# One-hot factors of the expert gates: eight tokens per instruction, in pairs of tokens, all on VectorE

## The chip, the cores and the metric

The kernel runs on one core of a Trainium2 chip. The metric is the device time of one execution in microseconds. Three runs of the kernel before gave 2724.03, 2725.5 and 2726.63 us (median 2725.5). All times below that are not totals come from one profiled execution of it.

## The reference, cut to what matters

The program is a two-layer transformer over 256 latent tokens and 256 context tokens. Each layer ends in a mixer of experts ("PEER"): for each token, eight heads pick 16 of 128 x 128 single-neuron experts, so that a token has 128 picks, each with an expert number and a gate.

```python
idx = (i1 * PEER_NKEYS + i2).reshape(T, PEER_HEADS * PEER_TOPK)
g = jax.nn.softmax(fv, axis=-1).reshape(T, PEER_HEADS * PEER_TOPK)
...
ue = u[ic]
ve = v[ic]
act = jax.nn.gelu(jnp.einsum('td,ted->te', hc, ue), approximate=False)
return jnp.einsum('te,ted->td', gc * act, ve)
```

i1 and i2 are the first and the second key of an expert, each 0 to 127. The kernel gathers rows of u and v for only 128 of the layer-0 tokens. For the other tokens (384 in layer 0, 256 in layer 1) it computes all 16384 experts densely, and multiplies by a dense table of gates that is zero where a token didn't pick an expert.

## The kernel before, in words

That dense table is made by `dense_gates`, once for each block of 128 tokens: three passes in layer 0, two in layer 1. For one token the table of 128 x 128 gates is a product of two matrices over the token's 128 picks: one row per pick that is one-hot in the second key (tile `oh2`, from i2), and one row per pick that holds the pick's gate at the place of the first key and zero elsewhere (tiles `go`). The gate is kept as two bf16 parts, x = 0 and x = 1, so each token takes two matmuls of 128x128 that add up in PSUM.

The first key's one-hot row is itself an outer product: n1 = 8 a + b, with a from 0 to 15 and b from 0 to 7. `one_hots(b)` makes, for 16 tokens, the one-hot of a (`hot0`, line 707), the one-hot of b (`hot1`, line 707), and `gh` = one-hot of a times either part of the gate (line 711). In `hot0`, `hot1` and `gh` the 16 tokens are the innermost dimension. Then for each group of eight tokens line 723 makes `oh2` in one VectorE instruction of 1024 elements per partition (four pairs of tokens x 128 keys x 2), and line 730 makes `go` by four instructions for each gate part, one for each pair of tokens, 256 elements per partition each. It reads two adjacent tokens out of every 16 of `hot1`. The instructions of part x = 1 go to GpSimd for the first `pools` groups of every 16 tokens, which `SHARE` sets by block: two of two in the first pass, none in the second, third and fifth, one of two in the fourth. That is 96 instructions on GpSimd and 544 on VectorE.

TensorE does the 16 matmuls of eight tokens (line 739) into two PSUM banks, ScalarE copies each bank to the tile `stage` (line 741), and after 16 tokens SyncE's queue writes `stage` to HBM as 1 MB (line 742). `oh2`, `go` and `stage` have two buffers each.

The five passes don't run alone. `dense` is the loop over the 128 rows of experts. Its first half, `first(i)`, loads 512 KB of u, splits it into two bf16 parts (ScalarE line 100, VectorE line 101), projects all tokens onto it with 24 matmuls (line 281) and applies Gelu (line 766). The results of the first 28 rows in layer 0 and the first 48 in layer 1 have places to be kept (four more buffers rotate), so these `first` steps may run while the gates are still being made. The second half, `second(i)`, needs the finished table (tile `gq`, read back from HBM). The routing of the next block (`route`: lines 620 to 670, all on VectorE) also lies within a pass. The order of all instructions on an engine is set at build time by a scheduler that works with its own estimate of costs; at run time every engine goes through its own list in order.

Of the kernel before, what the change touches and what calls it, by code (L numbers as in the profile page):

```python
# [10 lines left out]
BF = mybir.dt.bfloat16  # L11
# [22 lines left out]
NK = 128  # L34
# [7 lines left out]
TB = 16  # L42
OCT = 8
OHT = 8


@with_exitstack
def program(ctx: ExitStack, tc: tile.TileContext, a, out):
    nc = tc.nc
    V, A, T, G = nc.vector, nc.scalar, nc.tensor, nc.gpsimd  # L50
# [624 lines left out]
    def iota_tables(gp):  # L675
        row = load("iota", [P, NK], a["iota"], pool=gp)
        t = gp.tile([P, NK, 2], BF, name="iotaT")
        V.tensor_copy(t, row.unsqueeze(2).to_broadcast([P, NK, 2]))
        t16 = gp.tile([P, 16, TB], BF, name="iota16T")
        V.tensor_copy(t16, row[:, :16].unsqueeze(2).to_broadcast([P, 16, TB]))  # L680
        return t, t16

    def dense_gates(ii, gate, tb0, gd, gp, tables, steps, pools=2):
# [17 lines left out]
        def one_hots(b):  # L701

            bs = slice(b * TB, (b + 1) * TB)
            hot = []
            for x, n in ((0, 16), (1, 8)):
                o = gp.tile([P, n, TB], BF, name=f"hot{x}", bufs=2)
                V.tensor_tensor(o, iota16[:, :n], iT[:, x, bs].unsqueeze(1).to_broadcast([P, n, TB]), op=OP.is_equal)
                hot.append(o)
            gh = gp.tile([P, 2, 16, TB], BF, name="gh", bufs=2)
            for x in range(2):  # L710
                V.tensor_tensor(gh[:, x], hot[0], gT[:, x, bs].unsqueeze(1).to_broadcast([P, 16, TB]), op=OP.mult)  # L711
            return hot[1], gh

        ahead = one_hots(0)
        for b in range(P // TB):
            stage = gp.tile([P, NK, TB], F32, name="stage", bufs=2)
            (low, gh), ahead = ahead, one_hots(b + 1) if b < P // TB - 1 else None
            for t8 in range(TB // OHT):

                ts = slice(b * TB + t8 * OHT, b * TB + (t8 + 1) * OHT)  # L720
                pairs = [P, OHT // 2, NK, 2]
                oh = gp.tile(pairs, BF, name="oh2", bufs=2)
                V.tensor_tensor(oh, iota.unsqueeze(1).to_broadcast(pairs),  # L723
                                iT[:, 2, ts].rearrange("p (q t) -> p q t", t=2).unsqueeze(2).to_broadcast(pairs), op=OP.is_equal)
                go = []
                for x in range(2):
                    o = gp.tile([P, OHT // 2, 16, 8, 2], BF, name=f"go{x}", bufs=2)
                    for q in range(OHT // 2):
                        t = t8 * OHT + 2 * q
                        (G if x == 1 and t8 < pools else V).tensor_tensor(  # L730
                            o[:, q], gh[:, x, :, t:t + 2].unsqueeze(2).to_broadcast([P, 16, 8, 2]),
                            low[:, :, t:t + 2].unsqueeze(1).to_broadcast([P, 16, 8, 2]), op=OP.mult)
                    go.append(o.rearrange("p q a b t -> p q (a b) t"))
                for t4 in range(0, OHT, 4):
                    p = bank(("sc", "pv")[t4 // 4])
                    for t in range(4):
                        q, r = (t4 + t) // 2, t % 2
                        for x in range(2):
                            T.matmul(p[:, t * NK:(t + 1) * NK], oh[:, q, :, r], go[x][:, q, :, r], start=(x == 0), stop=(x == 1))  # L739
# [92 lines left out]
    with ExitStack() as layer0:  # L832
        with ExitStack() as es:
# [8 lines left out]
            with tc.issue_after(mod_last[0].ins):  # L842
                r = rms_of((CTXS, XS))
# [3 lines left out]
            steps = modulation(0, (2, 3, 4), sc, f0, f0)  # L847
# [24 lines left out]
        for g in range(2):  # L872
            p = bank("tr")
# [4 lines left out]
        gd = tc.dram_tile([P, NK // OCT, 3 * P // TB, OCT * TB], F32, name="gd0")  # L878
        with ExitStack() as gstack:
            gp = pool("gates0", gstack, 1, side="right")  # L880
            tables = iota_tables(gp)
            picks = []
            advance(route(best[2], rp, rank, rp, "", picks), 13)
            advance(ctx_scores, 1)
            advance(x_scores, 6)
            for b, after in ((2, 0), (0, 1), (1, 3)):
                following = []
                steps = route(best[after], rp, rank, *((keep, "3") if after == 3 else (rp, "")), following)
                dense_gates(*picks, b * P // TB, gd, gp, tables, chain(x_scores, steps), SHARE[b])
# [107 lines left out]
    with ExitStack() as layer1:  # L997
# [13 lines left out]
        with ExitStack() as gstack:  # L1011
            gp = pool("gates1", gstack, 1, side="right")
            tables = iota_tables(gp)
            picks, following = [], []
            advance(route(best[0], rp, rank, rp, "", picks), 13)
            advance(scores, 1)
            dense_gates(*picks, 0, gd, gp, tables, route(best[1], rp, rank, rp, "", following), SHARE[3])
            dense_gates(*following, P // TB, gd, gp, tables, iter(()), SHARE[4])
        right.close()
        dp = pool("dp1", layer1, 2, side="right")  # L1020

# [153 lines left out]
```

## Time and profile before

| | us |
|---|---|
| median of three runs | 2725.5 |
| the profiled execution | 2726.53 |
| its span in the trace | 2724.8 |
| layer 0: first, second, third pass of the gates (533 to 643, 643 to 723, 723 to 796) | 110, 80, 73 |
| layer 1: first, second pass (1987 to 2094, 2094 to 2163) | 107, 69 |

The span runs from the first instruction to the last; the 1.7 us between it and the execution's time lie outside of the trace. The boundaries of the stretches are read from the chain of waits: a pass begins with its first `oh2` and its last stretch ends when its gates are written. A busy time adds up the time in which at least one instruction of a group runs. Since two VectorE instructions overlap a little where one follows the other directly, the step from one start to the next is shorter than a duration; the pieces of the chain show these steps.

### The profile page before, as it was taken

The numbers are of one execution on the slowest core, as the hardware profiler recorded it, in microseconds if no ns is written. First come the engines' busy times: TensorE is split into PE (matmuls) and PEld (weight loads), VectorE is DVE, ScalarE is ACT, GpSimd is POOL, SyncE is SP. The second block draws the span as 40 slices with busy tenths as digits, with TensorE's granted clock in tenths as the row PEclk, the third lists the DMA queues.
The fourth block names the chain that finished last, engine by engine and source line by source line (L and its number), as shares of the span: only waits on it lengthen the run. The fifth ranks groups of instructions, "written<-read, shape, count | busy, mean of one in ns | idle before, by whom it ended". The sixth has DMA issues, their size and how long they took to land.

```text
span 2724.8 us, 42285 instructions
## 1 busy us (share of the span) xinstructions
PE 2490.9 (91%) x15465; PEld 1588.5 (58%) x15600; DVE 2246.9 (82%) x5284; ACT 1222.3 (45%) x2117; POOL 317.4 (12%) x228
## 2 busy tenths in 40 slices
PE   6999999989559999999999998898988599999998
PEld 2866489655334455555555555667877444666665
DVE  6975659999999999999898886967998897666665
ACT  3235535434333443344443334555554345555554
POOL 0000000160000122332322210000043000000000
PEclk8989899989659999999999999899999699999999
DMA  7621225455569899999999863603566787767762
GB/s 259 220 75 36 87 99 178 128 163 171 147 232 350 327 370 369 359 400 382 373 363 356 332 220 117 222 1 101 175 188 200 238 284 266 245 218 233 233 218 84
DMA packets 221005, 614.13 MB, mean 225 GB/s; under 512 B 16758, under 2 KB 104312, under 8 KB 199804
## 3 DMA queue, kind: packets, MB, share of 16 engines
q1 hardware_dynamic: 202364, 477.19, 51.4%
q0 software_dynamic: 18432, 134.23, 12.6%
q8 instruction: 122, 2.00, 0.3%
q14 instruction: 87, 0.71, 0.1%
HBM read 565.21 MB, written 46.15 MB: 224 GB/s over the span
## 4 chain that ended last, share of the span: by engine, by line
PE 66%; DVE 24%; DMA 4%; issue 3%; ACT 2%; POOL 1%; SPq 0%; DVEq 0%; ACTq 0%; POOLq 0%
PE tr L281 21%; PE sc L789 10%; PE pv L789 10%; PE mm L281 7%; DVE go L730 6%; PE mm L789 6%; DVE half L101 5%; DMA v<-in_v 2%; PE sc L384 2%; DVE oh L723 2%; PE tr L291 1%; PE pv L548 1%; PE mm L319 1%; PE sc L531 1%; PE sc L319 1%
## 5 line engine op out<-in xcount | busy, mean ns | idle before, releaser
L281 PEld LDWEIGHTS <-half 128*128 128x128 bf16 x7488 | 727.3, 99 | 291.9 <-issue 15.2
L281 PE MATMUL tr<-h,half 128*128 128x384 bf16 (+1 forms) x6144 | 885.4, 301 | 3.2 <-ACT ga L766 1.6
L789 PEld LDWEIGHTS <-wh 128*128 128x128 bf16 x2560 | 251.0, 98 | 317.3 <-ACT wh L781 35.2
L101 DVE TENSOR_TENSOR half<-u,half 128x1024 bf16<-128x1024 f32 (+1 forms) x300 | 368.9, 1231 | 70.2 <-ACT half L100 69.6
L774 DVE TENSOR_TENSOR vv<-v,vv 128x1024 bf16<-128x1024 f32 x256 | 312.0, 1220 | 98.0 <-ACT vv L773 97.4
L773 ACT ACTIVATE vv<-v 128x1024 bf16<-128x1024 f32 x256 | 268.9, 1054 | 259.2 <-DMA v<-in_v 84.6
L100 ACT ACTIVATE half<-u 128x1024 bf16<-128x1024 f32 (+1 forms) x300 | 315.0, 1050 | 100.7 <-DMA u<-in_u 36.2
L907 POOL DMA_INDIRECT uv<-in_uv,idx x128 | 201.2, 1572 | 780.9 <-DVE acc L919 458.8
L789 PE MATMUL pv<-vv,wh 128*128 128x512 bf16 x956 | 255.0, 381 | 40.5 <-ACT wh L781 33.8
L789 PE MATMUL sc<-vv,wh 128*128 128x512 bf16 x994 | 266.2, 381 | 2.0 <-issue 0.4
L766 ACT ACTIVATE ga<-tr 128x384 f32<-128x384 f32 (+1 forms) x230 | 100.1, 435 | 307.9 <-PE tr L281 305.1
L730 POOL TENSOR_TENSOR go<-gh,hot 128x256 bf16<-128x256 bf16 x96 | 116.0, 1239 | 976.8 <-DVE gh L711 932.3
L789 PEld LDWEIGHTS <-wl 128*128 128x128 bf16 x1280 | 125.4, 98 | 151.0 <-issue 0.8
L159 DVE CUSTOM_DVE_ANT_0 junk<-wm,silu_c 128x1024 bf16<-128x1024 f32 x160 | 194.6, 1216 | 4.1 <-DMA wm<-in_w_mod 3.1
L730 DVE TENSOR_TENSOR go<-gh,hot 128x256 bf16<-128x256 bf16 x544 | 191.9, 413 | 0.0
L779 DVE TENSOR_TENSOR wf<-ga,gq 128x384 f32<-128x384 f32 (+1 forms) x230 | 111.6, 489 | 92.8 <-ACT ga L766 81.0
L739 PEld LDWEIGHTS <-oh 128*128 128x128 bf16 x1280 | 106.5, 114 | 133.2 <-DVE oh L723 42.9
L781 ACT ACTIVATE wh<-wf 128x384 bf16<-128x384 f32 (+1 forms) x256 | 117.8, 462 | 144.5 <-DVE wf L779 93.0
L919 DVE SCALAR_TENSOR_TENSOR acc<-uv,wgt,acc 128x1024 f32<-128x1024 f32 x127 | 162.4, 1279 | 1.9
L913 DVE CUSTOM_DVE_ANT_0 uv<-uv,ht 128x1024 f32<-128x1024 f32 x128 | 155.4, 1215 | 2.7 <-DMA uv<-in_uv,idx 2.7
L789 PE MATMUL pv<-vv,wl 128*128 128x512 bf16 x508 | 152.0, 380 | 0.3
L789 PE MATMUL sc<-vv,wl 128*128 128x512 bf16 x508 | 151.4, 379 | 0.2
(274 smaller groups left out, 3005.3 us busy)
## 6 DMA issues: line engine op xcount, KB each, us to landing
u<-in_u SPq DMA_DIRECT2D x256, 512.0 KB
v<-in_v SPq DMA_DIRECT2D x256, 512.0 KB
wm<-in_w_mod SPq DMA_DIRECT2D x80, 512.0 KB
gd<-stage SPq DMA_DIRECT2D x40, 1024.0 KB
gq<-gd SPq DMA_DIRECT2D x16, 1536.0 KB
gq<-gd SPq DMA_DIRECT2D x16, 1024.0 KB
u<-in_w_pq SPq DMA_DIRECT2D x24, 512.0 KB
v<-in_w_pq SPq DMA_DIRECT2D x24, 512.0 KB
```

The costliest lines, as they stand in the source:

```text
L100: A.activation(h, t, AF.Copy)
L101: V.tensor_tensor(l, t, h, op=OP.subtract)
L159: mod_last[0] = order(V.tensor_tensor_reduce(junk, w, sc[:, s], 1.0, 0.0, OP.mult, OP.add, mods[layer][:, k, j, s:s + 1]))
L281: T.matmul(p[:, :n], w[i][:, c], src[j][:, c, t0:t0 + n], start=(c == 0 and i + j == 0), stop=(c == NC - 1 and i == 1))
L730: (G if x == 1 and t8 < pools else V).tensor_tensor(o[:, q], gh[:, x, :, t:t + 2].unsqueeze(2).to_broadcast([P, 16, 8, 2]), low[:, :, t:t ...
L773: A.activation(vh, v, AF.Copy)
L774: V.tensor_tensor(vl, v, vh, op=OP.subtract)
L781: A.activation(wh, wf, AF.Copy)
L789: T.matmul(acc[t][x], w[:, s], v[:, x * 512:(x + 1) * 512], start=(i == 0 and w is wh and v is vh), stop=(i == NK - 1 and w is wl))
L907: dma = G.indirect_dma_start(out=uv[:], out_offset=None, in_=a["uv0"], in_offset=bass.IndirectOffsetOnAxis(ap=idx[:, k:k + 1], axis=0))
L913: keep_order(V.tensor_tensor_reduce(uv[:, :D], uv[:, :D], ht, 1.0, 0.0, OP.mult, OP.add, act3[:, k:k + 1]))
L919: V.scalar_tensor_tensor(acc3, uv[:, D:], wgt3[:, k:k + 1], acc3, op0=OP.mult, op1=OP.add)
```

## The change

`one_hots(n)` now works for 32 tokens (`QUART`) and in five-dimensional tiles. `gh` is laid out as groups of eight tokens: [group, a, token]; its one-hot of a is written in place and multiplied there, so three instructions of 512 elements per partition replace the six of 256 that 32 tokens took (`hot0` and `gh`). The one-hot of b, now `low`, is laid out as [pair of tokens, b, token of the pair], by one instruction of 256 elements for 32 tokens. `go` is one tile for both gate parts, and each part of eight tokens comes from one instruction of 1024 elements. That instruction goes through a, the pairs, b and the token of a pair; it reads the eight tokens' part of `low` as one run of 64 elements, again for each a, and writes runs of 16 elements that lie 256 elements apart. All of them are on VectorE; `SHARE` and `pools` go. The one-hots are no longer made one block of 16 tokens ahead in the code. Matmuls, copies and writes are the same.

```diff
-        t16 = gp.tile([P, 16, TB], BF, name="iota16T")
-        V.tensor_copy(t16, row[:, :16].unsqueeze(2).to_broadcast([P, 16, TB]))
+        t16 = gp.tile([P, 16, OHT], BF, name="iota16T")
+        V.tensor_copy(t16, row[:, :16].unsqueeze(2).to_broadcast([P, 16, OHT]))
...
-            hot = []
-            for x, n in ((0, 16), (1, 8)):
-                o = gp.tile([P, n, TB], BF, name=f"hot{x}", bufs=2)
-                V.tensor_tensor(o, iota16[:, :n], iT[:, x, bs].unsqueeze(1).to_broadcast([P, n, TB]), op=OP.is_equal)
-                hot.append(o)
-            gh = gp.tile([P, 2, 16, TB], BF, name="gh", bufs=2)
-            for x in range(2):
-                V.tensor_tensor(gh[:, x], hot[0], gT[:, x, bs].unsqueeze(1).to_broadcast([P, 16, TB]), op=OP.mult)
-            return hot[1], gh
...
+            ns = slice(n * QUART, (n + 1) * QUART)
+            wide, pairs = [P, QUART // OHT, 16, OHT], [P, QUART // 2, 8, 2]
+            group = lambda x: x.rearrange("p (g t) -> p g t", t=OHT).unsqueeze(2).to_broadcast(wide)
+            gh = gp.tile([P, 2] + wide[1:], BF, name="gh", bufs=2)
+            V.tensor_tensor(gh[:, 0], iota16.unsqueeze(1).to_broadcast(wide), group(iT[:, 0, ns]), op=OP.is_equal)
+            V.tensor_tensor(gh[:, 1], gh[:, 0], group(gT[:, 1, ns]), op=OP.mult)
+            V.tensor_tensor(gh[:, 0], gh[:, 0], group(gT[:, 0, ns]), op=OP.mult)
+            low = gp.tile(pairs, BF, name="low", bufs=2)
+            V.tensor_tensor(low, iota[:, :8].unsqueeze(1).to_broadcast(pairs),
+                            iT[:, 1, ns].rearrange("p (q t) -> p q t", t=2).unsqueeze(2).to_broadcast(pairs), op=OP.is_equal)
+            return gh, low
...
-                    o = gp.tile([P, OHT // 2, 16, 8, 2], BF, name=f"go{x}", bufs=2)
-                    for q in range(OHT // 2):
-                        t = t8 * OHT + 2 * q
-                        (G if x == 1 and t8 < pools else V).tensor_tensor(
-                            o[:, q], gh[:, x, :, t:t + 2].unsqueeze(2).to_broadcast([P, 16, 8, 2]),
-                            low[:, :, t:t + 2].unsqueeze(1).to_broadcast([P, 16, 8, 2]), op=OP.mult)
-                    go.append(o.rearrange("p q a b t -> p q (a b) t"))
+                    V.tensor_tensor(go[:, x].rearrange("p q (a b) t -> p a q b t", b=8),
+                                    gh[:, x, g].rearrange("p a (q t) -> p a q t", t=2).unsqueeze(3).to_broadcast(outer),
+                                    low[:, g * nq:(g + 1) * nq].unsqueeze(1).to_broadcast(outer), op=OP.mult)
```

The scheduler's lists change with it. On VectorE, in the middle of the third pass, eight tokens stand as follows before. The names are those of the code, with `oh` for the one-hot of the second key and `fv`, `fi`, `rest` of the routing of the next block:

```order
L730 TENSOR_TENSOR go_6860<-gh,hot_6713 128x256
L723 TENSOR_TENSOR oh_6858<-iotaT,iT 128x1024
L730 TENSOR_TENSOR go_6860<-gh,hot_6713 128x256 x3
L730 TENSOR_TENSOR go_6865<-gh,hot_6713 128x256 x2
L630 MAX_INDEX fi<-fv,rest_6613 128x8
L730 TENSOR_TENSOR go_6865<-gh,hot_6713 128x256 x2
```

In the changed kernel sixteen tokens of the same pass stand like this (`gh` and `low` here are the next 32 tokens' one-hots, the lines 637 and 651 the routing):

```order
L728 TENSOR_TENSOR oh_6458<-iotaT,iT 128x1024
L733 TENSOR_TENSOR go<-gh,low 128x16x4x16 x2
L637 TENSOR_REDUCE gs<-gate 128x8
L709 TENSOR_TENSOR gh<-iota16T,iT 128x512
L713 TENSOR_TENSOR low<-iotaT,iT 128x256
L651 CAST atf<-at 128x128
L728 TENSOR_TENSOR oh_6483<-iotaT,iT 128x1024
L733 TENSOR_TENSOR go<-gh,low 128x16x4x16 x2
```

Eight `go` instructions of eight tokens became two; the scheduler still makes the next 32 tokens' one-hots before they are due. On VectorE in the last pass, 16 tokens before (line 101 is the split of u for two `first` steps):

```order
L723 TENSOR_TENSOR oh_20219<-iotaT,iT 128x1024
L730 TENSOR_TENSOR go_20221<-gh,hot_20141 128x256 x3
L730 TENSOR_TENSOR go_20226<-gh,hot_20141 128x256 x4
L723 TENSOR_TENSOR oh_20251<-iotaT,iT 128x1024
L730 TENSOR_TENSOR go_20253<-gh,hot_20141 128x256 x4
L730 TENSOR_TENSOR go_20258<-gh,hot_20141 128x256 x4
L707 TENSOR_TENSOR hot_20358<-iota16T,iT 128x256
L101 TENSOR_TENSOR half<-u_23491,half 128x1024
L101 TENSOR_TENSOR half<-u_23546,half 128x1024
```

And now:

```order
L728 TENSOR_TENSOR oh_19614<-iotaT,iT 128x1024
L733 TENSOR_TENSOR go<-gh,low 128x16x4x16 x2
L728 TENSOR_TENSOR oh_19639<-iotaT,iT 128x1024
L733 TENSOR_TENSOR go<-gh,low 128x16x4x16 x2
L102 TENSOR_TENSOR half<-u_22771,half 128x1024
L709 TENSOR_TENSOR gh<-iota16T,iT 128x512
L713 TENSOR_TENSOR low<-iotaT,iT 128x256
```

The splits of u keep their places between the groups: from the first `oh2` of a pass to that of the next, or to the table's end, VectorE's list holds 16, 11, 0, 25 and 10 of them before, and 18, 9, 0, 24 and 11 now. TensorE's list holds 386 and 183 of the 128x384 projections in the first two passes before, 429 and 118 now, none in the third in either; in the fourth pass 571 of the 128x256 ones before and 544 now.

## Rows read from the trace of the kernel before

**Rows 1.** The page: busy time, share of the span and instruction count of each engine over the whole program, and the granted TensorE clock in 40 equal slices of the span, in tenths of full speed.

```profile
PE 2490.9 (91%) x15465; PEld 1588.5 (58%) x15600; DVE 2246.9 (82%) x5284; ACT 1222.3 (45%) x2117; POOL 317.4 (12%) x228
...
PEclk8989899989659999999999999899999699999999
```

**Rows 2.** Five stretches, which are the five passes of dense_gates with what lies in front of them. Columns: the stretch and its length in us; busy us (and instructions) of PE, PEld, DVE, ACT and POOL; granted TensorE clock as a share of full speed; mean busy share of the DMA engines; GB/s.

```profile
533.00:643.00 110.00, 94.12 (x664) 59.92 (x663) 109.79 (x364) 46.27 (x72) 59.45 (x64) 0.91 0.52 154
643.00:723.00 80.00, 60.99 (x466) 39.62 (x464) 79.90 (x251) 33.02 (x51) 0.00 (x0) 0.85 0.60 174
723.00:796.00 73.00, 36.20 (x258) 26.10 (x258) 72.67 (x277) 24.08 (x39) 0.00 (x0) 0.50 0.45 128
1987.00:2094.00 107.00, 87.71 (x816) 72.97 (x813) 97.28 (x233) 52.41 (x84) 56.56 (x32) 0.90 0.65 197
2094.00:2163.00 69.00, 52.79 (x483) 42.79 (x480) 66.70 (x188) 31.89 (x54) 0.00 (x0) 0.77 0.67 199
```

**Rows 3.** The chain of waits between 640 and 732 us: its shares by line, and five of its pieces in order of time (start us, us on the chain, engine, tile, line, and xN where N instructions follow each other).

```profile
by line: DVE go L730 45.9%; DVE half L101 12.5%; DVE oh L723 11.3%; DVE gh L711 4.3%; issue 3.5%; DVE hot L707 3.3%; DVE oh L669 2.5%; DVE oh L666 2.5%; DVE rest L628 1.7%; DVE fi L630 1.6%; DVE fi L627 1.6%; DVE oh L665 1.3%; DVE fv L626 1
...
641.92 0.53 DVE hot L707 x3
...
644.50 1.14 DVE half L101
645.63 0.60 DVE gh L711 x3
...
711.72 0.60 DVE oh L723
712.32 2.70 DVE go L730 x9
```

**Rows 4.** The chain of waits between 1984 and 2168 us, the passes of layer 1: its shares by line, and the last write of gates to HBM.

```profile
by line: DVE go L730 33.0%; DVE half L101 15.3%; POOL go L730 10.0%; DVE oh L723 9.4%; PE tr L281 9.2%; issue 4.7%; DVE gh L711 3.4%; DVE hot L707 3.3%; DMA gd<-stage 2.9%; PE sc L739 1.9%; PE pv L739 1.8%; DVE fi L627 0.8%; DVE fi L630 0.7
...
2162.15 5.25 DMA gd<-stage
```

**Rows 5.** VectorE's groups by line between 533 and 623 us, the first pass. Columns: line, engine, operation, out<-in, shapes, count | busy us, mean ns of one | idle us before.

```profile
L730 DVE TENSOR_TENSOR go<-gh,hot 128x256 bf16<-128x256 bf16 x64 | 31.4, 536 | 0.0
L101 DVE TENSOR_TENSOR half<-u,half 128x1024 bf16<-128x1024 f32 x12 | 16.5, 1375 | 0.0
L723 DVE TENSOR_TENSOR oh<-iotaT,iT 128x1024 bf16<-128x1024 bf16 x16 | 12.2, 762 | 0.0
L711 DVE TENSOR_TENSOR gh<-hot,gT 128x256 bf16<-128x256 bf16 x16 | 7.8, 520 | 0.0
L707 DVE TENSOR_TENSOR hot<-iota16T,iT 128x128 bf16<-128x128 bf16 (+1 forms) x13 | 5.7, 442 | 0.0
```

**Rows 6.** The same columns for VectorE between 1987 and 2094 us, the fourth pass.

```profile
L730 DVE TENSOR_TENSOR go<-gh,hot 128x256 bf16<-128x256 bf16 x96 | 37.5, 443 | 0.0
L101 DVE TENSOR_TENSOR half<-u,half 128x1024 bf16<-128x1024 f32 x25 | 32.5, 1305 | 9.6 <-ACT half L100 9.6
L723 DVE TENSOR_TENSOR oh<-iotaT,iT 128x1024 bf16<-128x1024 bf16 x16 | 11.2, 706 | 0.0
L707 DVE TENSOR_TENSOR hot<-iota16T,iT 128x256 bf16<-128x256 bf16 (+1 forms) x14 | 4.9, 353 | 0.0
L711 DVE TENSOR_TENSOR gh<-hot,gT 128x256 bf16<-128x256 bf16 x16 | 3.8, 277 | 0.0
```

**Rows 7.** Instructions in order of time around 2055 us, merged: start us, us, engine, line, operation, count [idle before <- what ended it].

```profile
2055.18 20.23 POOL L730 TENSOR_TENSOR go<-gh,hot 128x256 bf16<-128x256 bf16 x4 [5.85 <-DVE gh L711]
...
2073.63 1.08 PE L739 MATMUL sc<-go,oh 128*128 128x128 bf16 x7 [8.83 <-POOL go L730]
...
2079.47 1.22 DVE L101 TENSOR_TENSOR half<-u,half 128x1024 bf16<-128x1024 f32 x1 [6.41 <-ACT half L100]
```

**Rows 8.** Line 730 over the whole program: engine, operation, count: duration in ns, shortest/median/longest, first and last start.

```profile
L730 DVE TENSOR_TENSOR go<-gh,hot x544: 327/381/847, 536.9 to 2160.3; 128x256 bf16<-128x256 bf16 x182
L730 POOL TENSOR_TENSOR go<-gh,hot x96: 642/802/18402, 535.3 to 2074.8; 128x256 bf16<-128x256 bf16 x96
```

**Rows 9.** TensorE's groups by line and shape between 533 and 643 us, columns as in rows 5.

```profile
L281 PE MATMUL tr<-h,half 128*128 128x384 bf16 x388 | 70.6, 342 | 0.0
L739 PE MATMUL pv<-go,oh 128*128 128x128 bf16 x128 | 13.6, 241 | 6.0 <-DVE go L730 5.9
L739 PE MATMUL sc<-go,oh 128*128 128x128 bf16 x128 | 13.1, 241 | 9.9 <-DVE oh L723 5.1 <-DVE go L730 4.6
```

**Rows 10.** TensorE in order of time between 639 and 653 us, merged (start us, us, count); a group of eight matmuls can show seven here, the other one standing apart or missing.

```profile
639.67 7.15 PE L281 MATMUL tr<-h,half 128*128 128x384 bf16 x43
...
651.11 0.64 PE L739 MATMUL pv<-go,oh 128*128 128x128 bf16 x7
651.72 0.63 PE L739 MATMUL sc<-go,oh 128*128 128x128 bf16 x7
```

**Rows 11.** The same for the fifth pass, in layer 1.

```profile
2104.04 4.53 PE L281 MATMUL tr<-h,half 128*128 128x256 bf16 x40
```

**Rows 12.** ScalarE's split of the streamed u weights (line 100) between 1987 and 2094 us, columns as in rows 5.

```profile
L100 ACT ACTIVATE half<-u 128x1024 bf16<-128x1024 f32 x24 | 25.3, 1054 | 19.9 <-DMA u<-in_u 14.5 <-DVE go L730 2.2 <-DVE gh L711 2.1
```

More of the change, by code (lines that the diff above doesn't have):

```diff
@@ L44 @@
 OHT = 8
+QUART = 32
 @with_exitstack
@@ L678, in iota_tables, with dense_gates @@
         V.tensor_copy(t, row.unsqueeze(2).to_broadcast([P, NK, 2]))
-        t16 = gp.tile([P, 16, TB], BF, name="iota16T")
-        V.tensor_copy(t16, row[:, :16].unsqueeze(2).to_broadcast([P, 16, TB]))
+        t16 = gp.tile([P, 16, OHT], BF, name="iota16T")
+        V.tensor_copy(t16, row[:, :16].unsqueeze(2).to_broadcast([P, 16, OHT]))
         return t, t16
-    def dense_gates(ii, gate, tb0, gd, gp, tables, steps, pools=2):
+    def dense_gates(ii, gate, tb0, gd, gp, tables, steps):
         iota, iota16 = tables
@@ L699, in dense_gates @@
         V.tensor_tensor(gT[:, 1], p[:, 3 * P:], gT[:, 0], op=OP.subtract)
-        def one_hots(b):
-            bs = slice(b * TB, (b + 1) * TB)
-            hot = []
-            for x, n in ((0, 16), (1, 8)):
-                o = gp.tile([P, n, TB], BF, name=f"hot{x}", bufs=2)
-                V.tensor_tensor(o, iota16[:, :n], iT[:, x, bs].unsqueeze(1).to_broadcast([P, n, TB]), op=OP.is_equal)
-                hot.append(o)
-            gh = gp.tile([P, 2, 16, TB], BF, name="gh", bufs=2)
-            for x in range(2):
-                V.tensor_tensor(gh[:, x], hot[0], gT[:, x, bs].unsqueeze(1).to_broadcast([P, 16, TB]), op=OP.mult)
-            return hot[1], gh
@@ L714, in dense_gates, with one_hots @@
-        ahead = one_hots(0)
+        def one_hots(n):
+            ns = slice(n * QUART, (n + 1) * QUART)
[9 more added lines that the diff above has]
+            return gh, low
@@ L715, in dense_gates @@
+        nq = OHT // 2
         for b in range(P // TB):
             stage = gp.tile([P, NK, TB], F32, name="stage", bufs=2)
-            (low, gh), ahead = ahead, one_hots(b + 1) if b < P // TB - 1 else None
+            if b % (QUART // TB) == 0:
+                gh, low = one_hots(b // (QUART // TB))
             for t8 in range(TB // OHT):
[L720 to L725, printed above, removed]
-                for x in range(2):
-                    o = gp.tile([P, OHT // 2, 16, 8, 2], BF, name=f"go{x}", bufs=2)
-                    for q in range(OHT // 2):
-                        t = t8 * OHT + 2 * q
-                        (G if x == 1 and t8 < pools else V).tensor_tensor(
-                            o[:, q], gh[:, x, :, t:t + 2].unsqueeze(2).to_broadcast([P, 16, 8, 2]),
-                            low[:, :, t:t + 2].unsqueeze(1).to_broadcast([P, 16, 8, 2]), op=OP.mult)
-                    go.append(o.rearrange("p q a b t -> p q (a b) t"))
@@ new lines, in dense_gates @@
+                g = b * (TB // OHT) + t8
+                ts = slice(g * OHT, (g + 1) * OHT)
+                g %= QUART // OHT
+                shape = [P, nq, NK, 2]
+                oh = gp.tile(shape, BF, name="oh2", bufs=2)
+                V.tensor_tensor(oh, iota.unsqueeze(1).to_broadcast(shape),
+                                iT[:, 2, ts].rearrange("p (q t) -> p q t", t=2).unsqueeze(2).to_broadcast(shape), op=OP.is_equal)
+                go = gp.tile([P, 2] + shape[1:], BF, name="go", bufs=2)
@@ L734, in dense_gates @@
+                outer = [P, 16, nq, 8, 2]
+                for x in range(2):
+                    V.tensor_tensor(go[:, x].rearrange("p q (a b) t -> p a q b t", b=8),
+                                    gh[:, x, g].rearrange("p a (q t) -> p a q t", t=2).unsqueeze(3).to_broadcast(outer),
+                                    low[:, g * nq:(g + 1) * nq].unsqueeze(1).to_broadcast(outer), op=OP.mult)
                 for t4 in range(0, OHT, 4):
@@ L738, in dense_gates @@
                         for x in range(2):
-                            T.matmul(p[:, t * NK:(t + 1) * NK], oh[:, q, :, r], go[x][:, q, :, r], start=(x == 0), stop=(x == 1))
+                            T.matmul(p[:, t * NK:(t + 1) * NK], oh[:, q, :, r], go[:, x, q, :, r], start=(x == 0), stop=(x == 1))
                     ts0 = t8 * OHT + t4
@@ L820, in program @@
     PRE = (18, 32)
-    SHARE = {2: 2, 0: 0, 1: 0, 3: 1, 4: 0}
     PARKED = (TT * NC // (3 * P), TT * NC // SEQ)
@@ L888, in program @@
                 steps = route(best[after], rp, rank, *((keep, "3") if after == 3 else (rp, "")), following)
-                dense_gates(*picks, b * P // TB, gd, gp, tables, chain(x_scores, steps), SHARE[b])
+                dense_gates(*picks, b * P // TB, gd, gp, tables, chain(x_scores, steps))
                 picks = following
@@ L1016, in program @@
             advance(scores, 1)
-            dense_gates(*picks, 0, gd, gp, tables, route(best[1], rp, rank, rp, "", following), SHARE[3])
-            dense_gates(*following, P // TB, gd, gp, tables, iter(()), SHARE[4])
+            dense_gates(*picks, 0, gd, gp, tables, route(best[1], rp, rank, rp, "", following))
+            dense_gates(*following, P // TB, gd, gp, tables, iter(()))
         right.close()
```

## The prediction

> **What bounds the kernel now.** I read the page first. Over the whole program TensorE is busy 91% and VectorE 82% [rows 1], which names TensorE; but the change touches only the five passes that make the gates, so I cut these out by windows. [...] In layer 1 line 730 has 33%, GpSimd's share of the same line 10% and TensorE's projections 9% [rows 4]. [...]
>
> **Prices.** On the bounding engine I count from one start to the next, as the chain does: `go` 2.70 / 9 = 0.30 us, `oh2` 0.60, `gh` 0.60 / 3 = 0.20, `hot` 0.53 / 3 = 0.18, a split of u 1.14 [rows 3]. A duration is some 0.08 us more, since neighbours overlap.
>
> The new `go` has 1024 bf16 elements, as `oh2` has. `oh2` too holds a pair of one source over many steps, reads the other as a run and takes 0.60. I take 0.60, the nearest row; it is the lower end too, as no two-source row passes more elements in a time. The upper end is one element at a time: the split of u, also 1024 elements but partly fp32, 1.14.
>
> What speaks for the dearer end is that the old `go` takes 0.30 where `gh`, of the same size and type, takes 0.20 [rows 3]: something in its access costs 0.10 us over 128 pairs. [...] No run here has yet shown which of the streams pays.
>
> The one-hots of 512 elements aren't in the trace. They lie between 0.20 (256) and 0.60 (1024); on the line between these 0.33. The ends would change a pass by -1.6 or +3.2 us.
>
> **One pass, VectorE alone.** Before, without GpSimd: 128 `go` x 0.30 + 16 `oh2` x 0.60 + 16 `gh` x 0.20 + 16 `hot` x 0.18 = 38.4 + 9.6 + 3.2 + 2.9 = 54.1. After: 32 x 0.60 + 16 x 0.60 + 12 x 0.33 + 4 x 0.20 = 19.2 + 9.6 + 4.0 + 0.8 = 33.6. That is 20.5 us less.
>
> **What VectorE then needs, pass by pass** (the new list has 18, 9, 0, 24 and 11 splits of u where there were 16, 11, 0, 25 and 10).
> - First: GpSimd had half of `go`, but everything on VectorE ran longer beside it: 64 `go` at 536 ns, `gh` at 520, `oh2` at 762, splits at 1375 [rows 5], where the median of all `go` is 381 [rows 8]. The four groups' 57.1 us less 109 overlaps of 0.08 are 48.4; 33.6 replace them, -14.8. The splits fall back to 1.22: 12 x 0.155 = -1.9. Two more splits: +2.3. 110 - 14.4 = 95.6.
> - Second: 80 - 20.5 - 2 x 1.14 = 57.2. Third: 73 - 20.5 = 52.5.
> - Fourth: 57.4 us in the four groups less 142 x 0.08 are 46.0 [rows 6], so -12.4; splits 25 x 0.085 = -2.1; one split less -1.1. Here one GpSimd `go` lasted 18.4 us, 0.64 at best [rows 8]: TensorE stood 8.8 us for it and VectorE afterwards 6.4 in one piece [rows 7], 9.6 in all [rows 6]. That goes too: 107 - 25.2 = 81.8.
> - Fifth: 69 - 20.5 + 1.1 = 49.6.
>
> **What is late next.** TensorE's work doesn't shrink. A 128x384 projection takes 7.15 / 43 = 0.166 us at the full clock, a 128x256 one 4.53 / 40 = 0.113, eight gate matmuls 0.61 from one group's start to the next [rows 10, 11], so a pass's 32 groups 19.5. First pass: the new list's 429 projections x 0.166 + 19.5 = 91; before, their 70.6 us and the gates' 27 filled most of the 110 [rows 9]. Second 39, third 20 (39 at half clock), fourth 544 x 0.113 + 19.5 = 81, fifth 264 x 0.113 + 19.5 = 49. In the second and third VectorE stays alone. In the first, fourth and fifth the two are equal within 5%, and two engines that feed each other through two buffers don't both run full.
>
> The transfers come closer as well. In the fourth pass ScalarE already waits 14.5 us for u [rows 12] at a DMA share of 0.65 [rows 2]; in 90 us that share is 0.77. At the end of the fifth pass no split is left, VectorE needs 33.6 / 8 = 4.2 us for 16 tokens, and the write of their 1 MB takes 5.25 us [rows 4] out of two buffers: I let three or four such groups take a microsecond more each.
>
> So I take 98 (95.6 + 2), 58, 53, 90 (82 + 8 for u and TensorE) and 57 (50 + 4 for the writes + 3 for u): 356 us instead of 439, 83 less. What is behind the passes has the same matmuls in the same number but for a projection step or two, and is TensorE's [rows 1]; I count nothing there. The profiled execution took 2726.5 us (1.0 above the median of 2725.5): 2726.5 - 83 = **2643 us**.
>
> GpSimd's 96 instructions cost nothing by their absence; its gathers come later and aren't moved. ScalarE and the copies are as before. The loss of the written look-ahead costs nothing where the list has the next one-hots early, as it has; where it hasn't, two or three dependent instructions per 32 tokens wait for each other, within the "issue" share of 3.5% [rows 3].
>
> **The rivals.**
> - *VectorE's sum is all there is.* The scheduler's list happens to keep TensorE and u in step: 95.6 + 57.2 + 52.5 + 81.8 + 49.6 = 337, -102, 2624 us. For it: TensorE has filled such stretches well. Against it: three passes with two equal limits. 14%.
> - *Layer 1 gives nothing,* because u, the 1 MB writes and TensorE hold it where it is: 98 + 58 + 53 + 107 + 69 = 385, -54, 2672 us. For it: the 14.5 us wait, TensorE busy 88 of 107. Against it: most of that busy time is matmuls in a pipeline that waits, and the 18 us GpSimd instruction goes anyway. 16%.
> - *One element at a time:* `go` at 1.14 adds 160 x 0.54 = 86; some 17 of that are hidden under the allowances above: 2726.5 - 83 + 86 - 17 = 2712. Against it `oh2`, which has the same dimensions. 5%.
> - *Slower: the hop price on every stream.* If the 0.10 us per 128 pairs is paid by both sources and the output (whose runs are 256 elements apart), 512 pairs pay 3 x 0.40, `go` costs 1.80, and 160 x 1.20 - 17 = 175 more give 2818. The change loses from `go` = 0.60 + (83 + 17) / 160 = 1.22 on. For it: the old price is unexplained by the trace. Against it: `gh` and `oh2` are free of it. 4%.
> - *Nothing moves:* the passes wait for something that the chain doesn't name, within 0.2% of before. 2%.
>
> **How the numbers follow.** My forecast, 2626 to 2662 (the allowances halved or doubled), has 59%. The range takes in the two neighbours: 2610 to 2685; what is left out is mainly the dear `go` and luck beyond. Two runs of this kernel can be told apart by about 0.2%, 5.5 us. Faster by more: 59 + 14 + 16 + 5 = 94%; within: 2%; slower: 4%.
>
> **What would show it.** Right: `go` x160 at about 660 to 680 ns; `gh` at 0.40 or so; nothing of line 730's successor on GpSimd; the third pass, free of projections, at 53 us with VectorE full; the first and fourth with both engines over 90%. Wrong: `go` above 0.8; a third pass above 60, which would mean that dependences between VectorE and TensorE and not VectorE's work set it; TensorE idle behind u in layer 1; a dense stage that became longer by what the passes gave.

## The result and the profile after

The changed kernel takes 2623.8 us (median of four runs, 2620.2 to 2627.2) where the kernel before, on the same chips, takes 2725.1: a ratio of 0.9626, with a 95% interval of 0.9614 to 0.9638. That is 101 us less. The forecast was 2643 us within 2610 to 2685; the measured time lies on the first rival, VectorE's bare sum of 2624.

The page, beside [rows 1]: busy time by engine, and the granted clock in 40 slices.

```profile
PE 2454.3 (94%) x15600; PEld 1570.8 (60%) x15600; DVE 2142.3 (82%) x4820; ACT 1218.7 (46%) x2117; POOL 196.4 (7%) x132
...
PEclk8989899999679999999999999999999899999999
```

TensorE's share rises from 91 to 94% because the span is shorter; GpSimd's busy time falls by the 116 us of `go` and a little more. The stretch of the third pass, which stood at a granted 0.50 in [rows 2], has 0.61 in the window below.

The five passes by windows, beside [rows 2], same columns. The cuts are put at the new places of each pass's first `oh2`:

```profile
534.00:625.00 91.00, 88.30 (x708) 59.07 (x706) 90.86 (x321) 47.69 (x75) 0.00 (x0) 1.00 0.66 198
625.00:686.00 61.00, 49.84 (x430) 35.73 (x428) 60.90 (x168) 31.07 (x51) 0.00 (x0) 0.86 0.68 201
686.00:738.00 52.00, 29.06 (x256) 23.99 (x256) 49.91 (x139) 20.96 (x35) 0.00 (x0) 0.61 0.66 186
1928.00:2010.00 82.00, 79.24 (x825) 70.82 (x824) 75.05 (x155) 50.86 (x84) 0.00 (x0) 0.98 0.83 257
2010.00:2066.00 56.00, 42.83 (x477) 38.18 (x475) 50.24 (x80) 32.89 (x54) 0.00 (x0) 0.91 0.87 264
```

VectorE is still full in layer 0, and TensorE is at 88 of 91 us beside it in the first pass. In the fourth and fifth VectorE stands for 7 and 6 us, and the DMA share has gone from 0.65 and 0.67 to 0.83 and 0.87.

The new `go` over the whole program, beside [rows 8] (count: shortest/median/longest ns), and the first of the three instructions that make `gh`:

```profile
L733 DVE TENSOR_TENSOR go<-gh,low x160: 673/682/692, 539.8 to 2056.2; 128x1024 bf16<-128x1024 bf16 x160
```

```profile
L709 DVE TENSOR_TENSOR gh<-iota16T,iT x20: 397/412/424, 534.0 to 2039.3; 128x512 bf16<-128x512 bf16 x20
```

160 instructions at a median of 682 ns, where `oh2` has 681 for as many elements, and 512 elements in 412 ns: the prices 0.60 and 0.33 from start to start that the forecast used. The chain at the end of the third pass shows the steps, beside [rows 3] (start us, us on the chain, piece):

```profile
by line: DVE go L733 35.7%; DVE oh L728 17.7%; DMA gq<-gd 12.8%; DMA gd<-stage 10.8%; DVE fi L631 2.9%; DVE gh L709 2.4%; DVE gh L710 2.4%; DVE gh L711 2.3%; DVE rest L629 2.1%; DVE oh L670 2.1%; DVE oh L667 2.1%; DVE oh L666 2.1%; ACT stag
...
726.32 0.60 DVE oh L728
726.92 1.21 DVE go L733 x2
728.32 0.60 DVE oh L728
728.92 1.22 DVE go L733 x2
...
732.24 5.81 DMA gd<-stage
738.11 6.94 DMA gq<-gd
```

Two `go` are 1.20 to 1.22 us, `oh2` 0.60. The pass now ends with the last write and the read back, where VectorE's routing used to be the last thing.

For a comparison pass by pass I use the same cuts everywhere: from a pass's first `oh2` to the next pass's first `oh2`, and for the third and fifth to the issue of the first read of `gq`. "Sum" is the forecast's bare VectorE sum (-14.4, -22.8, -20.5, -25.2, -19.4) on these cuts.

| pass | before, us | sum, us | after, us |
|---|---|---|---|
| 1 | 109.5 | 95.1 | 90.0 |
| 2 | 82.4 | 59.6 | 61.8 |
| 3 | 69.0 | 48.5 | 51.5 |
| 4 | 108.3 | 83.1 | 81.9 |
| 5 | 72.3 | 52.9 | 55.7 |
| all | 441.5 | 339.2 | 340.9 |

So 100.6 us of the 102.5 by which the span shrank come from these passes. Between them and behind them nothing was given back: from the first read of `gq` in layer 0 to the first `oh2` of layer 1 it is 1193.4 us before and 1190.7 after.

### The profile page after: what moved, and what is told of

Its sections match the earlier page's. It is cut to its first block, busy times and chain, and to the rows that moved or that the text cites. A ratio compares the mean times of both kernels' runs of the same rounds, so it can differ in the third digit from the quotient of the medians.

```text
span 2622.3 us, 41821 instructions
## 1 busy us (share of the span) xinstructions
PE 2454.3 (94%) x15600; PEld 1570.8 (60%) x15600; DVE 2142.3 (82%) x4820; ACT 1218.7 (46%) x2117; POOL 196.4 (7%) x132
## 4 chain that ended last, share of the span: by engine, by line
PE 71%; DVE 19%; DMA 5%; issue 2%; ACT 2%; SPq 0%; DVEq 0%; ACTq 0%
PE tr L282 23%; PE sc L791 12%; PE pv L791 12%; PE mm L282 8%; PE mm L791 6%; DVE half L102 4%; DVE go L733 3%; PE sc L385 2%; PE tr L292 2%; DVE oh L728 1%; PE pv L549 1%; PE mm L320 1%; PE sc L320 1%; PE sc L532 1%; DMA u<-in_u 1%
## 5 line engine op out<-in xcount | busy, mean ns | idle before, releaser
L791 PE MATMUL pv<-vv,wh 128*128 128x512 bf16 x1024 | 269.7, 382 | 35.2 <-ACT wh L783 32.1
L282 PE MATMUL mm<-h,half 128*128 128x256 bf16 (+1 forms) x1248 | 137.4, 271 | 11.1 <-ACT h L274 3.5
L282 PE MATMUL mm<-hT,half 128*128 128x512 f32 (+1 forms) x672 | 140.1, 362 | 6.6 <-ACT hT L274 3.1
L791 PE MATMUL mm<-vv,wh 128*128 128x512 bf16 x512 | 134.4, 381 | 0.0
```

The lines of the kernel that those rows point to most:

```text
L282: T.matmul(p[:, :n], w[i][:, c], src[j][:, c, t0:t0 + n], start=(c == 0 and i + j == 0), stop=(c == NC - 1 and i == 1))
L791: T.matmul(acc[t][x], w[:, s], v[:, x * 512:(x + 1) * 512], start=(i == 0 and w is wh and v is vh), stop=(i == NK - 1 and w is wl))
```

## The experiments

Nine kernels were run. All medians are of runs beside the kernel before on the same chip, which took 2726.3 to 2727.3 us there.

### GpSimd's part alone

The kernel before, with all of line 730 on VectorE:

```diff
-    SHARE = {2: 2, 0: 0, 1: 0, 3: 1, 4: 0}
+    SHARE = {2: 0, 0: 0, 1: 0, 3: 0, 4: 0}
```

> The kernel before with all of line 730 on VectorE and nothing else changed. Theory A (the gain is VectorE's own: the price of one go): the first pass gains 64 go x 0.30 on VectorE and loses GpSimd's interference, 54.1 in place of 48.4 and splits 1.9 less, +4; the fourth 54.1 in place of 46.0, splits 2 less, the 9.6 us stall gone, -4. In all 2725 us, within 8. Rival B (what the change won is mostly GpSimd's interference and its 18 us instruction): 40 to 60 us of the 101 come from this alone, 2665 to 2685.

Measured 2712.5 us, ratio 0.9956 (0.9942 to 0.9970): 14 us faster than the kernel before. That is far from rival B, but 12 us below theory A's 2725 and outside the 8 that it allowed. The duration of `go` hardly moves against [rows 8], while VectorE does 96 more of them:

```profile
L730 DVE TENSOR_TENSOR go<-gh,hot x640: 330/385/475, 535.3 to 2148.9; 128x256 bf16<-128x256 bf16 x160
```

The passes tell where. The scheduler's list now has 21, 6, 0, 26 and 9 splits of u in the passes. With 1.14 us for each split more or less and the price of `go` as forecast, they should take 119.0, 76.7, 69.0, 105.8 and 71.2 us; measured are 114.4, 76.6, 69.1, 102.1 and 71.1. Passes two, three and five agree within 0.1 us. The first and fourth, the two with GpSimd, are 4.6 and 3.7 us shorter than reckoned: the forecast had taken VectorE's work beside GpSimd too low (why is said further down).

```profile
535.00:649.00 114.00, 103.72 (x768) 66.43 (x767) 113.76 (x432) 51.77 (x80) 0.00 (x0) 1.00 0.57 171
1987.00:2089.00 102.00, 90.48 (x875) 76.06 (x873) 97.97 (x267) 53.42 (x88) 0.00 (x0) 0.98 0.72 217
```

The windows of these two passes show VectorE full at 113.8 of 114 us and 98.0 of 102 even without it (columns as in [rows 2]). In the fourth it still waits 4.0 us behind u:

```profile
L101 DVE TENSOR_TENSOR half<-u,half 128x1024 bf16<-128x1024 f32 x26 | 31.2, 1213 | 4.0 <-ACT half L100 4.0
```

### GpSimd's part given back to the changed kernel

```diff
-                    V.tensor_tensor(go[:, x].rearrange("p q (a b) t -> p a q b t", b=8),
+                    (G if x == 1 and t8 < pools else V).tensor_tensor(go[:, x].rearrange("p q (a b) t -> p a q b t", b=8),
```

with `pools` from the old `SHARE`.

> The changed kernel with GpSimd's old share back: all of part x = 1 in the first pass (16 big go), half of it in the fourth (8). VectorE loses 9.6 and 4.8 us of work. Theory A with interference as measured before (VectorE's instructions ran 19 us longer in the first pass beside 59 us of GpSimd): a big go on GpSimd takes at least 4 x 0.64 = 2.6 us, 16 of them 41, so 14 us are lost for 9.6 won there, and the fourth loses a few too: 2628 to 2640 us. Rival: GpSimd is free help and its removal cost something: 2612 to 2618.

Measured 2638.9 us, ratio 0.9676 (0.9659 to 0.9694): 15 us slower than the changed kernel, as theory A had it. The first pass by groups (all engines; busy us, mean ns):

```profile
L733 POOL TENSOR_TENSOR go<-gh,low 128x1024 bf16<-128x1024 bf16 x16 | 38.3, 2408 | 566.0 <-DVE gh L710 542.6 <-PE pv L741 11.6 <-DVE gh L711 4.5
...
L102 DVE TENSOR_TENSOR half<-u,half 128x1024 bf16<-128x1024 f32 x17 | 26.5, 1556 | 0.0
...
L733 DVE TENSOR_TENSOR go<-gh,low 128x1024 bf16<-128x1024 bf16 x16 | 12.5, 784 | 0.0
L728 DVE TENSOR_TENSOR oh<-iotaT,iT 128x1024 bf16<-128x1024 bf16 x16 | 12.3, 775 | 0.0
```

VectorE's own instructions run longer beside GpSimd: splits at 1556 ns instead of 1214 in the changed kernel, `go` at 784 instead of 685, `oh2` at 775 instead of 681. The pass took 97.7 us. It should have been 90.0 - 9.6 (16 `go` gone) - 2.3 (two splits fewer), 78.1; so 38.3 us of GpSimd cost 19.6. In the fourth pass one GpSimd instruction starved again:

```profile
L733 POOL TENSOR_TENSOR go<-gh,low x24: 1922/2338/13964, 533.6 to 1998.2; 128x1024 bf16<-128x1024 bf16 x24
```

13.96 us where the median is 2.34, as with the 18.4 us in [rows 8]. It started at 1982.32 us, and 18 VectorE instructions, one close behind the other, ran at their usual length while it lasted; it ended 1.8 us after the last of them. With the next GpSimd `go` it was the other way round: VectorE's `go` started 0.51 us later, took 2.42 us and ended 0.55 us behind it.

```profile
1998.23 2.38 POOL L733 TENSOR_TENSOR go<-gh,low 128x1024 bf16<-128x1024 bf16 x1 [1.95 <-PE pv L741]
1998.74 2.42 DVE L733 TENSOR_TENSOR go<-gh,low 128x1024 bf16<-128x1024 bf16 x1
```

So either engine's instruction was drawn out beside the other's in this run: GpSimd's to 13.96 us, VectorE's to 2.42 where the median is 0.68. But the 18 VectorE instructions all started after GpSimd's, as the one of 2.42 us did, and yet were not held up by it; what decides which of the two is held up stays open.

### Four small instructions with the new layout

This separates the layout from the size of the instruction:

```diff
-                    V.tensor_tensor(go[:, x].rearrange("p q (a b) t -> p a q b t", b=8),
-                                    gh[:, x, g].rearrange("p a (q t) -> p a q t", t=2).unsqueeze(3).to_broadcast(outer),
-                                    low[:, g * nq:(g + 1) * nq].unsqueeze(1).to_broadcast(outer), op=OP.mult)
+                    for q in range(nq):
+                        V.tensor_tensor(go[:, x, q].rearrange("p (a b) t -> p a b t", b=8),
+                                        gh[:, x, g, :, 2 * q:2 * q + 2].unsqueeze(2).to_broadcast([P, 16, 8, 2]),
+                                        low[:, g * nq + q].unsqueeze(1).to_broadcast([P, 16, 8, 2]), op=OP.mult)
```

> The changed kernel, but each part of eight tokens again by four instructions of 256 elements, reading the new layouts (pairs of tokens, low as a run of 16 elements), all on VectorE. Theory H (the old go paid for reading hot1 as single pairs far apart): a go takes 0.20 from start to start like gh of the same size, a pass costs 128 x 0.20 = 25.6 in place of 19.2, 5 x 6.4 = 32 over the changed kernel: 2656 us, and line 730's successor has a duration of about 280 ns. Rival I (the old price is that of so many short instructions, whatever they read): 0.30 each, 128 x 0.30 = 38.4, 5 x 19.2 = 96 over: 2720 us, duration about 380 ns.

Measured 2646.1 us, ratio 0.9712 (0.9696 to 0.9728).

```profile
L734 DVE TENSOR_TENSOR go<-gh,low x640: 242/285/311, 536.4 to 2081.4; 128x256 bf16<-128x256 bf16 x160
```

From start to start, in the third pass:

```profile
713.85 1.62 DVE go L734 x8
```

285 ns instead of 385 for the same 256 elements, 0.20 us from start to start instead of 0.30: theory H's price, and within 10 us of its time. The old price was not that of a short instruction but of what it read. Of the way from 2712 to 2624 us the layout (with the one-hots in fewer instructions) makes 66 and the merging of four into one 22.

### Which distance between pairs costs

Three kernels vary only how the one-hot of b lies in memory. First in the changed kernel, with every pair of tokens followed by two unused elements, so that the big `go` reads single pairs 8 bytes apart:

```diff
-            low = gp.tile(pairs, BF, name="low", bufs=2)
+            low = gp.tile(pairs[:3] + [4], BF, name="low", bufs=2)[:, :, :, :2]
```

> The changed kernel with the one-hot of b stored with two unused elements behind every pair, so that the one big go reads 64 single pairs 8 bytes apart instead of one run of 64 elements; all else the same. Theory H: 512 pairs pay 0.10 us per 128, 0.60 + 0.40 = 1.00 us each, duration near 1080 ns, 160 x 0.40 = 64 more of VectorE's time: 2675 to 2690 us (the writing of low pays a little too). Rival I (runs don't matter, the number of instructions does): 0.60, 2624 us. A third outcome, a price above 1.00, would mean that small steps cost more than the 32 bytes of before.

Measured 2620.6 us, ratio 0.9618 (0.9602 to 0.9634), no dearer than the changed kernel.

```profile
L733 DVE TENSOR_TENSOR go<-gh,low x160: 677/686/709, 537.1 to 2053.8; 128x1024 bf16<-128x1024 bf16 x160
```

A miss for theory H as it stood: 686 ns against 682. Single pairs at this distance cost nothing that can be seen. So in the kernel of four small instructions (285 ns) I put back the old layout, 16 tokens innermost, in which a pair lies 32 bytes from the next, and one with eight tokens innermost, 16 bytes:

```diff
-            low = gp.tile(pairs, BF, name="low", bufs=2)
+            low = gp.tile([P, QUART // TB, 8, TB], BF, name="low", bufs=2)
...
-                                        low[:, g * nq + q].unsqueeze(1).to_broadcast([P, 16, 8, 2]), op=OP.mult)
+                                        low[:, g // 2, :, g % 2 * OHT + 2 * q:g % 2 * OHT + 2 * q + 2].unsqueeze(1).to_broadcast([P, 16, 8, 2]), op=OP.mult)
```

> The kernel of four small instructions again (2646 us, 285 ns each), with the one-hot of b laid out with 16 tokens innermost, so that go reads it as before: single pairs 32 bytes apart; gh keeps its new layout. It costs one small instruction of 128 elements more per 32 tokens, some 3 us in all. Theory H, narrowed by the run with pairs 8 bytes apart, which cost nothing (a pair that lies 32 bytes from the next one is what costs): 0.30 from start to start, 385 ns, 640 x 0.10 = 64 us more, near 2713. Rival J (the price was in how gh was read, held pairs 32 bytes apart, which this kernel doesn't have): 285 ns, 2649 us.

> The same kernel of four small instructions with the one-hot of b in groups of eight tokens, so that go reads single pairs 16 bytes apart. If the price grows with the distance up to 32 bytes, something between 285 and 385 ns, 2650 to 2700 us; if it sets in at 32 bytes alone, or rival J holds, 285 ns and 2646 us; if it sets in at 16 already, 385 ns and 2710 us.

At 32 bytes 2713.8 us, ratio 0.9950 (0.9934 to 0.9965), at 16 bytes 2700.8, ratio 0.9906 (0.9890 to 0.9921). Their `go`, 32 bytes first:

```profile
L737 DVE TENSOR_TENSOR go<-gh,low x640: 337/396/462, 535.0 to 2150.8; 128x256 bf16<-128x256 bf16 x160
```

```profile
L735 DVE TENSOR_TENSOR go<-gh,low x640: 356/402/516, 536.6 to 2137.0; 128x256 bf16<-128x256 bf16 x160
```

And a piece of their chains from the second pass, in the same order:

```profile
710.40 2.40 DVE go L737 x8
```

```profile
709.08 2.31 DVE go L735 x8
```

At 32 bytes it is 0.30 us from start to start: the whole old price of 0.10 us for 128 pairs is back, though `gh` keeps its new layout. Rival J falls; the one-hot of b was the stream that paid. At 16 bytes it is 0.29, nearly as dear, though the duration is no shorter. The two times lie 13 us apart: 7.7 in the passes (some 5 by `go`, 2 by the additional small instruction) and 7 between the layers (1197.7 us and 1190.3), which was not taken apart. So single pairs in the second source paid at 16 and at 32 bytes, and those 8 bytes apart, at 686 ns against 682, did not. The 8-byte run differs from the others in the length of the instruction too, so where between 8 and 16 bytes the price begins, and whether the length matters, stays open.

The output's side, with `go` stored in the order in which it is computed:

```diff
-                go = gp.tile([P, 2] + shape[1:], BF, name="go", bufs=2)
+                go = gp.tile([P, 2, 16, nq, 8, 2], BF, name="go", bufs=2)
...
-                            T.matmul(p[:, t * NK:(t + 1) * NK], oh[:, q, :, r], go[:, x, q, :, r], start=(x == 0), stop=(x == 1))
+                            T.matmul(p[:, t * NK:(t + 1) * NK], oh[:, q, :, r], go[:, x, :, q, :, r], start=(x == 0), stop=(x == 1))
```

> The changed kernel with go stored in the order in which it is computed, [a, pair, b, token], so that the instruction writes one run of 1024 elements instead of 64 runs of 16 that lie 256 elements apart; TensorE reads it with one more step in its pattern. Theory H (runs of two or more pairs are free on every stream): go stays at 0.60 (680 ns), 2624 us within 5. Rival (the output's hops have a price too): go falls below 0.60, for 0.05 us each 8 us less, 2616 or lower; if TensorE's longer step costs something, its eight gate matmuls show more than 0.61 us and the time rises.

Measured 2619.4 us, ratio 0.9612 (0.9596 to 0.9628); its interval meets that of the changed kernel, and its passes take 341.5 us where those of the changed kernel take 340.8.

```profile
L733 DVE TENSOR_TENSOR go<-gh,low x160: 660/678/686, 535.5 to 2051.9; 128x1024 bf16<-128x1024 bf16 x160
```

678 ns against 682: writing runs of 16 elements 256 apart had no price that can be seen.

### Twice the new work

```diff
-                for x in range(2):
-                    V.tensor_tensor(go[:, x].rearrange("p q (a b) t -> p a q b t", b=8),
+                for again in range(2):
+                    for x in range(2):
+                        V.tensor_tensor(go[:, x].rearrange("p q (a b) t -> p a q b t", b=8),
```

> The changed kernel with every go instruction made twice (the second writes the same values again): 160 x 0.60 = 96 us more work on VectorE, nothing else. Theory A (VectorE's sum still sets all five passes in the changed kernel): every pass is 19.2 us longer, 2720 us. Rival C (TensorE, u and the writes set the first, fourth and fifth pass, as the forecast's allowances of 2, 8 and 7 us said): these passes absorb 17 or more before they grow, 2703 us or less, and the second and third alone grow by the full 19.2.

Measured 2727.2 us, ratio 1.0006 (0.9997 to 1.0016): 103 us more than the changed kernel for 96 us of work. Nothing was absorbed, so rival C falls; the 7 us beyond the 96 were not expected. Its windows (columns as in [rows 2]):

```profile
534.00:651.00 117.00, 113.86 (x865) 74.30 (x862) 116.90 (x355) 55.63 (x87) 0.00 (x0) 1.00 0.62 185
651.00:724.00 73.00, 30.35 (x260) 26.63 (x260) 72.97 (x204) 21.90 (x37) 0.00 (x0) 0.63 0.41 116
724.00:800.00 76.00, 30.04 (x256) 26.50 (x256) 67.19 (x158) 21.45 (x36) 0.00 (x0) 0.56 0.48 135
1994.00:2109.00 115.00, 104.93 (x1040) 92.65 (x1038) 107.21 (x198) 63.49 (x102) 0.00 (x0) 0.97 0.73 225
2109.00:2174.00 65.00, 29.61 (x256) 26.44 (x256) 56.99 (x100) 21.84 (x35) 0.00 (x0) 0.53 0.54 156
```

The passes are 117.2, 73.8, 74.8, 114.9 and 64.2 us. That the second and fifth grow by only 12.0 and 8.5 is the scheduler's doing: its list has 25, 2, 0, 35 and 0 splits of u instead of 18, 9, 0, 24 and 11. The changed kernel's passes plus 19.2 and 1.14 for each split moved give 117.2, 73.0, 70.7, 113.6 and 62.4. VectorE's work sets each pass, to 4 us or less; the largest rest is that of the third.

### Both gate parts in one instruction

A line through the 0.20 us from start to start that 256 elements took and the 0.60 of 1024 leaves 0.067 us for an instruction of any length. By this estimate 80 instructions less save 5 us where VectorE sets the passes, which I took as 2614 to 2620 us. For this `gh` was laid out as [group, part, a, token] and `go` as [pair, part, key, token], so that part and a become one step in every pattern:

```diff
-                for x in range(2):
-                    V.tensor_tensor(go[:, x].rearrange("p q (a b) t -> p a q b t", b=8),
-                                    gh[:, x, g].rearrange("p a (q t) -> p a q t", t=2).unsqueeze(3).to_broadcast(outer),
-                                    low[:, g * nq:(g + 1) * nq].unsqueeze(1).to_broadcast(outer), op=OP.mult)
+                V.tensor_tensor(go.rearrange("p q x (a b) t -> p (x a) q b t", b=8),
+                                gh[:, g].rearrange("p x a (q t) -> p (x a) q t", t=2).unsqueeze(3).to_broadcast(outer),
+                                low[:, g * nq:(g + 1) * nq].unsqueeze(1).to_broadcast(outer), op=OP.mult)
```

> The changed kernel with both gate parts of eight tokens made by one instruction of 2048 elements (gh laid out by group, part, a, token; go by pair, part, key, token). [...] Rival: TensorE gets the first part 0.6 us later and loses it again, 2624 us or more.

Measured 2608.3 us, ratio 0.9562 (0.9549 to 0.9575): faster than both kernels, 15 us below the changed one and below the estimate's 2614 to 2620.

```profile
L732 DVE TENSOR_TENSOR go<-gh,low x80: 1208/1228/1270, 537.3 to 2041.7; 128x2048 bf16<-128x2048 bf16 x80
```

Its chain in the third pass:

```profile
698.46 1.14 DVE go L732
...
702.44 0.60 DVE oh L728
703.04 1.14 DVE go L732
```

1.14 from start to start for what two instructions did in 1.20, 5 us over 80. The passes are 8.1 us shorter in all (89.2, 60.8, 50.1, 76.9, 55.7); in the fourth VectorE also stands 2.6 us less than in the changed kernel, 4.3 instead of 6.9. The rest, some 6 us, lies outside of them: the first `oh2` comes 4.4 us earlier, and the stretch between the layers is 1.2 us shorter. The merged instruction isn't needed for the 4.4: in seven of the other eight kernels of this section the first `oh2` comes at 530.3 to 532.2 us too, where it is 530.5 here and 534.9 in the changed kernel. Why it does was not taken apart.

## Why the forecast was right, and where it was off

- **What bounds the passes.** Right: VectorE's work; it is the bounding engine of the prediction's prices, by [rows 2] and [rows 3]. Doubling `go` made the program longer by all of it, and the passes of several kernels follow from one price list (0.60 or 0.30 for `go`, 1.14 for a split) within a few us.
- **The price of `go`, 0.60.** Right: 682 ns, where `oh2` has 681 for as many elements, and 0.60 to 0.61 from start to start. Why the old `go` took 0.10 us more than `gh` the prediction leaves open, and 0.60 was the price of the nearest row. The runs put it down to `hot1`'s scattered pairs: with pairs 32 bytes apart an instruction of 256 elements takes 0.30 us from start to start, with the new layout 0.20. Pairs 8 bytes apart had no price in the long instruction (686 ns against 682).
- **The one-hots, 0.33.** Right: 412 ns, and mostly 0.32 to 0.34 us from start to start on the chain of the third pass.
- **What was off: "So I take 98, 58, 53, 90 and 57".** On the cuts of the table the five values stand for 97.5, 60.4, 49.0, 91.3 and 60.3 us, together 17.6 more than measured; the first and fourth make 17 of it. Two terms were mis-sized.
  - The first is "The four groups' 57.1 us less 109 overlaps of 0.08 are 48.4", and the 46.0 that were found in the same way in the fourth pass. The 57.1 are busy times, in which the overlap of two neighbours of one group is counted only once already: 64 `go` of 536 ns are 34.3 us, and their busy time in [rows 5] is 31.4. So these overlaps were taken off twice, and the rows end at 623 us with 13 of the pass's 16 `hot`. Summed from each start to the next, the four groups take 52.8 us in the first pass and 52.9 in the fourth. In the fourth a second error works the other way: the whole wait of 9.6 us was put down to GpSimd, and without GpSimd 4.0 of it remain. The run with `SHARE` at zero puts the gain 4.6 and 3.7 us higher than the forecast, which these account for but for 0.2 and 0.8 us.
  - The other is the allowances for TensorE, u and the writes, 18 us in all. With the first term corrected the bare sum is 90.5, 59.6, 48.5, 79.4 and 52.9, and the measured passes are off by -0.5, +2.2, +3.0, +2.5 and +2.8, together 10. In the last three VectorE stands 2 to 3 us longer than without GpSimd in the old layout (2.3, 6.9 and 6.2 us instead of 0.2, 4.0 and 3.8). In the second it doesn't stand: 20 more of the small instructions of the routing lie in that pass now, 2.0 us from start to start. The forecast had moved only the splits of u.
  - The range has a slip as well: 2626 isn't the sum with the allowances halved, which is 2634, but with nearly all of them gone.
- **What is late next.** Half right. In the fourth pass u is late as forecast; ScalarE's and VectorE's rows, beside [rows 12] and [rows 6]:

```profile
L101 ACT ACTIVATE half<-u 128x1024 bf16<-128x1024 f32 x24 | 25.4, 1058 | 23.9 <-DMA u<-in_u 16.4 <-DVE rest L629 2.8 <-DVE half L102 2.6
```

```profile
L102 DVE TENSOR_TENSOR half<-u,half 128x1024 bf16<-128x1024 f32 x24 | 29.1, 1216 | 6.9 <-ACT half L101 6.9
```

ScalarE waits 16.4 us for u instead of 14.5, and VectorE 6.9 us behind it, where it waited 4.0 without GpSimd in the old layout. In the fifth pass the writes appear, too:

```profile
L101 ACT ACTIVATE half<-u 128x1024 bf16<-128x1024 f32 x11 | 11.6, 1058 | 4.8 <-DMA u<-in_u 4.4 <-PE tr L282 0.3
...
L743 ACT ACTIVATE stage<-sc 128x512 f32<-128x512 f32 x16 | 9.5, 594 | 10.9 <-DMA gd<-stage 6.0 <-PE sc L741 4.9
```

6.0 us in which a copy waits for a buffer that is still being written to HBM. Those waits are real but small, since VectorE does other work in most of them. That TensorE, equal to VectorE within 5%, would cost something in the first pass, because two engines that feed each other through two buffers don't both run full, was an assumption of the author's and wrong here: TensorE is busy 88.3 of 91 us there at a granted clock of 1.00 and VectorE 90.9, and the pass, 90.0 us, is no longer than VectorE's corrected sum of 90.5.
- **GpSimd's removal costs nothing.** Right, and more: it is 14 us of the gain by itself.
- **The rivals.** "VectorE's sum is all there is" had 14% and gave 2624 us, the measured time. That it hits the total is partly luck, because two errors cancel: the sum was some 8 us too long by the work beside GpSimd and 10 too short by the waits and the routing. On the corrected sum the waits and the routing cost 10 us, about midway between the rival's nothing and the forecast's 18. "One element at a time" (`go` at 1.14), "the hop price on every stream" (1.80) and the layer that gives nothing are ruled out: `go` took 0.60, and layer 1's passes went from 180.6 to 137.6 us. "One element at a time" is the author's name for the 1.14 us of a split; how many elements VectorE passes at a time no run shows. Nor is it shown that most of TensorE's busy time in the fourth pass was "matmuls in a pipeline that waits": the old list's 571 projections x 0.113 and the gates' 19.5, both prices at a granted 1.00, are 84 of the 87.7 us in [rows 2].

## What to carry to other kernels

Where one engine is full and its lines set the stage, price its list from start to start and trust that sum; allow for the next limits only what the trace shows the bounding engine itself to stand, not what others wait. Where such a sum starts from busy times, mind that they count overlaps within a group only once. For bf16 work with two sources on VectorE look at the distance at which pairs of elements are read: here 16 or 32 bytes in the second source made an instruction of 256 elements take 0.29 and 0.30 us from start to start instead of 0.20, and the new layout was worth three times what merging the instructions was (66 and 22 us). Handing part of such work to GpSimd made the full engine slower, by 19.6 us for 38.3 us of GpSimd's time in one pass, which was more than the 9.6 us of `go` that it took off.

## What the runs showed of the hardware that I had not expected

Single bf16 pairs 8 bytes apart were read as fast as adjacent ones (686 and 682 ns for 1024 elements), pairs 16 bytes apart nearly as slowly as pairs 32 bytes apart (0.29 and 0.30 us from start to start for 256 elements, where adjacent pairs take 0.20). The 8 bytes were tried in the long instruction alone, the others in the short one alone. An output in runs of 32 bytes, 512 bytes apart, cost nothing that can be seen (682 against 678 ns). A single GpSimd instruction again lasted long, 13.96 us beside 18 VectorE instructions where its median is 2.34.
